# Operands of the seven products without the norm's root, two plain tiles, and two pairs of tiles in 256-column passes

## The chip, the cores and the metric

One NeuronCore of a Trainium2 chip runs the whole program. The metric is the device time of one execution in microseconds (us); lower is better. Engines are named as the profile names them: PE (TensorE, matmuls), PEld (its weight loads), DVE (VectorE), ACT (ScalarE), POOL (GpSimd) and SP (SyncE, which issues most transfers).

## What is computed

A block of two layers on 512 tokens of width 1024. Each layer has a feed-forward, a mixer (attention in the first, Mamba-2 in the second) and a second feed-forward, so that four feed-forwards run, numbered 0 to 3. The reference, cut:

```python
def rms_norm(x, g):
    y = x * lax.rsqrt(jnp.mean(x * x, axis=-1, keepdims=True) + EPS)
    return y * g

def swiglu(x, w_gate, w_up, w_down):
    return (jax.nn.silu(x @ w_gate) * (x @ w_up)) @ w_down

for i in range(2):
    x = x + 0.5 * swiglu(rms_norm(x, ffn1_norm[i]), ffn1_w_gate[i], ffn1_w_up[i], ffn1_w_down[i])
    h = rms_norm(x, mix_norm[i])
    x = x + (moba_mixer(h, ...) if i == 0 else mamba2_mixer(h, ...))
    x = x + 0.5 * swiglu(rms_norm(x, ffn2_norm[i]), ffn2_w_gate[i], ffn2_w_up[i], ffn2_w_down[i])
```

All is float32. The hidden width of a feed-forward is 2816 = 22 tiles of 128.

## The kernel before

**Layout.** x lies in SBUF as eight tiles x0 to x7 of 128 features by 512 tokens. A float32 product is made of three faster matmuls: each operand is split into a high part in the format fp32r and the rest (hi and lo), and hi x hi, hi x lo and lo x hi are added in PSUM. ACT makes hi (a copy, `high`), DVE makes lo (a subtraction, `low`). That holds for weights too: they come from DRAM into nine buffers of 128 x 1024 (`wraw`), and `halve_weights` splits each unit into `whi` and `wlo`, of which four of each exist.

**A plain tile** of a feed-forward (`plain`) makes gate and up of 128 hidden features: 8 tiles of K, times 2, times 3 matmuls of 512 columns. Its moving operands are `xhi` and `xlo`, which are x times the norm's gain; the norm's root r is put on the results, in `gated`.

**A pair** of tiles (`pair`) uses a scheme of Strassen's kind: the two tiles' gate and up weights, two halves of K, and two halves of the 512 tokens form 2 x 2 blocks, and seven products (A11, A12, A21-A22, -S2, A12-S2, A11-A21, A22) take the place of eight. Sums of weights are made by accumulating transfers that POOL issues (`add_term`, wraw<-wgu and wraw<-wraw). Sums of x are made on DVE by `Norm.spread` and `combined` (xa, xb, xd, xe) and split by `sided` into tiles `side`, which hold hi in 256 columns and lo in the next 256. A product runs in two passes: the weight's hi with all 512 columns of `side`, which leaves two parts in two PSUM banks that are added later, and the weight's lo with the first 256. The results are joined in tiles c1, c2, c4 and c5 (`read`, `joined`), and `gate` forms silu(gate) times up.

**Order.** Feed-forward i handles the first tiles as plain ones (six in feed-forward 0, four in the others, `GROUPS[i][0]`), then groups of two or three pairs. Between the products of a group's pairs stand the down-products (`down`) of the group before: eight, one for each x tile. The last group's down-products end the feed-forward; each adds to an x tile, after which `Norm.add` starts the next norm's work on that tile. `Norm.finish` sums the squares on PE, takes the power on POOL, and spreads r over the partitions as `rb` (PE, then ACT). In the kernel before, the operands of the pairs are scaled by r as well, so that `spread` begins with

```python
yield When(lambda: self.rb is not None)
```

**What sets the order of the instructions.** The program is put in order when it is built, by `Scheduler`: it keeps a clock for each engine and an estimated cost for each operation, and always places next the operation that could start first, ties going to the lower rank. The main line (tiles, pairs, mixers) is one task on PE, whose order is fixed. All engines run their lists in order. `Q.norm` is true from the seventh sum of squares until r is there, and a new accumulating transfer is not begun in that time; one that had passed this test earlier may still be placed in it. Weights are loaded in the order of the list `jobs`.

Of the kernel before, what the change touches and what calls it, by code (L numbers as in the profile page):

```python
# [25 lines left out]
KT = D // 128  # L26
# [17 lines left out]
ATTN = (("qk", 0), ("v", 0), ("qk", 1), ("qk", 2), ("qk", 3), ("v", 1), ("wo", 0), ("wo", 1))  # L44

SSM = (("x", 0), ("z", 0), ("x", 1), ("z", 1), ("x", 2), ("z", 2), ("x", 3), ("z", 3), ("out", 0), ("x", 4), ("z", 4), ("x", 5), ("z", 5),
       ("x", 6), ("x", 7), ("z", 6), ("z", 7), ("out", 1), ("out", 2), ("out", 3))
# [108 lines left out]
class Scheduler:  # L156
# [188 lines left out]
def trunk(ctx, tc, xT, pos, consts, cols, rows, wgu, wd, wqk, wv, wo, win, wz, wdt, wout, outT):  # L345
# [10 lines left out]
    sizes = {"slot": 53, "hs": 12, "sq": 6, "tiny": 40, "wraw": 9, "whi": 4, "wlo": 4}  # L356
# [67 lines left out]
    def ffn_order(i):  # L424

        order = list(range(*GROUPS[i][0]))
        for g in range(1, len(GROUPS[i])):
            a, b = GROUPS[i][g]
            pairs = [(j, j + 1) for j in range(a, b, 2)]
            n = 0  # L430
            for m, pair in enumerate(pairs):
                downs = []
                while n < KT * (m + 1) // len(pairs):
                    downs.append(("down", g - 1, n))
                    n += 1
                order.append((pair, downs))
        return order + [("down", len(GROUPS[i]) - 1, n) for n in range(KT)]
# [7 lines left out]

    def pair_jobs(i, pair, downs):

        (b11, b21), (b12, b22) = ((wgu[i, j, :, :1024], wgu[i, j, :, 1024:]) for j in pair)
        right = {"A11": (b11, None), "A12": (b21, None), "A21-A22": (b12, b11), "-S2": (b22, "A21-A22"),
                 "A12-S2": (b22, None), "A11-A21": (b12, b22), "A22": (b21, "-S2")}  # L450
        for nm in pair_order(downs):
            if isinstance(nm, tuple):
                down_job(i, nm)
            else:
                src, term = right[nm]
                job(src, step=2.78, total=2.78, whole=True, term=term, name=nm)

    def pair_order(downs):
        rest = iter(downs)
        order = [next(rest, None) if nm is None else nm for nm in PAIR]  # L460
        return [nm for nm in order if nm is not None] + list(rest)

    for l in range(2):
        for i in (2 * l, 2 * l + 1):
            if i == 1:
                for what, c in ATTN:
                    if what == "wo":
                        job(wo[c, 0])
                        job(wo[c, 1])
                    else:  # L470
                        wide_jobs(wqk[c] if what == "qk" else wv[c])
            if i == 3:
                for what, n in SSM:
                    if what == "x":
                        job(win[n, 0])
                        job(win[n, 1])
                    elif what == "z":
                        job(wz[n])
                    else:
                        job(wout[n, 0])  # L480
                        job(wout[n, 1])
# [134 lines left out]
    class Norm:  # L616


        def __init__(self, gain):
            self.gain = gain  # L620
# [4 lines left out]
            self.plain, self.spread_left = 0, 8  # L625
            self.left = {nm: [None] * 4 for nm in PAIR if nm}

        def add(self, k, first=False):
            self.there += 1
            spawn(self.operand(k), URGENT - 1 if first else 10 + k)  # L630
            spawn(self.square(k, first), 9 if k == KT - 1 and not first else 30 + k)
# [18 lines left out]
        def spread(self):  # L650


            yield When(lambda: self.rb is not None)
            for k in range(4):
                xa, xb = yield [slot("xa"), slot("xb")]
                Q.uses[xa.tensor.name] = Q.uses[xb.tensor.name] = 4
                for t, kk in ((xa, k), (xb, k + 4)):
                    op = V.scalar_tensor_tensor(t, x[kk], self.gain[:, kk:kk + 1], self.rb, op0=OP.mult, op1=OP.mult)
                    yield op.frees(*([self.rb] if kk == 7 and not self.plain else []))
                self.spread_left -= 2  # L660
                spawn(self.sided("A11", k, xa[:, :256], xa), 60)
                spawn(self.sided("A12", k, xb[:, :256], xb), 61)
                spawn(self.sided("A22", k, xb[:, 256:], xb), 66)
                spawn(self.combined(k, xa, xb), 62)

        def combined(self, k, xa, xb):
            d = yield slot("xd")
            Q.uses[d.tensor.name] = 4
            yield V.tensor_tensor(d[:, :256], xa[:, 256:], xb[:, 256:], op=OP.subtract).frees(xa, xb)
            spawn(self.sided("A21-A22", k, d[:, :256], d), 62)  # L670
            yield V.tensor_tensor(d[:, 256:], d[:, :256], xa[:, :256], op=OP.subtract).frees(xa, d)
            spawn(self.sided("-S2", k, d[:, 256:], d), 63)
            e = yield slot("xe")
            Q.uses[e.tensor.name] = 2
            yield V.tensor_tensor(e[:, :256], xb[:, :256], d[:, 256:], op=OP.add).frees(xb, d)
            spawn(self.sided("A12-S2", k, e[:, :256], e), 64)
            yield V.tensor_tensor(e[:, 256:], xa[:, :256], xa[:, 256:], op=OP.subtract).frees(xa)
            spawn(self.sided("A11-A21", k, e[:, 256:], e), 65)
# [63 lines left out]
    def ffn(i, nrm, done, midway=None):  # L742
        spawn(nrm.finish(), URGENT - 1)
        spawn(nrm.spread(), 60)
        h = {}

# [6 lines left out]
        def gated(pg, pu, j):  # L753
# [5 lines left out]
            nrm.plain -= 2  # L759
            yield op.frees(*([] if nrm.plain or nrm.spread_left else [nrm.rb]))  # L760
# [30 lines left out]
        def pair(j0, j1, downs, last):  # L791
# [12 lines left out]
            out = {}  # L804

            def product(nm, ps, first):
                p = place[nm]
# [17 lines left out]

            def parts(ps):
                v = ps.rearrange("p (o h c) -> p o h c", o=2, h=2)
# [5 lines left out]
            def gate(j, t, src):  # L833
                if j not in out:
# [3 lines left out]
                a = out[j][0][:, 256 * t:256 * t + 256]  # L838
                yield S.activation(a, src[:, :256], AF.Silu)
# [5 lines left out]
            def read(ps, nm, box):  # L845

                hh, hl = parts(ps)
                t = yield slot(nm)
                yield S.activation(both(t), hl, AF.Copy)
                yield V.tensor_tensor(both(t), hh, both(t), op=OP.add)  # L850
                box[nm] = t

            def joined(ps, nm, box, sign, done):
# [3 lines left out]
                for m, part in enumerate(parts(ps)):  # L857
# [4 lines left out]
                    yield op.frees(*([ps] if m and done else []))  # L862
# [16 lines left out]
            def c21(x):  # L879
                hh, hl = parts(x)  # L880
# [6 lines left out]
            for nm in order:  # L887
# [4 lines left out]
                elif nm == "A11":  # L892
                    x_ = yield bank("px", 2)
                    yield from product(nm, x_, True)
                    spawn(read(x_, "c1", box), 6)
                elif nm == "A12":
                    z_ = yield bank("pz", 2)
                    yield from product(nm, z_, True)
                    spawn(c11(z_), 6)
                elif nm == "A21-A22":  # L900
                    y_ = yield bank("py", 2)
# [36 lines left out]
        for what in ffn_order(i):  # L938
            if isinstance(what, int):
                yield from plain(what, what == GROUPS[i][0][1] - 1)  # L940
# [47 lines left out]
    def attention(nrm, done):  # L988
# [126 lines left out]
        def project(c, last):  # L1115

            for m in range(2):
                p = take(wo[c, m])
                for o in range(4):
# [4 lines left out]
                    for k in range(4):  # L1124
# [4 lines left out]
                        if n == KT - 1:  # L1129
# [11 lines left out]
        values_of = {0: {}, 1: {}}  # L1141
        for what, c in ATTN:
            if what == "wo":
                yield from project(c, c == 1)
# [9 lines left out]
    def mamba(nrm, done):  # L1154
# [79 lines left out]
        scaled_left = [6 * G]  # L1234

# [156 lines left out]
        def project(b, last):  # L1392

            for m in range(2):
                p = take(wout[b, m])
                for o in range(4):
# [4 lines left out]
                    for k in range(4):  # L1401
# [4 lines left out]
                        if n == KT - 1:  # L1406
# [20 lines left out]
        for i, (what, n) in enumerate(SSM):  # L1427
# [15 lines left out]
            else:  # L1443
                yield from project(n, n == 3)
# [23 lines left out]
    norms = [Norm(g) for g in gains]  # L1468
    for i, m in enumerate((0, 2, 3, 5)):
        norms[m].plain = 2 * GROUPS[i][0][1]  # L1470
# [105 lines left out]
```

## Time and profile before

| | |
|---|---|
| median of 3 runs | 2020.22 us (2019.89 to 2020.79) |
| the profiled execution | 2020.6 us, span on the core 2018.8 us, granted TensorE clock 1.00 |
| instructions | 28279 |
| matmuls | 10404 |
| DMA | 332.35 MB, mean 165 GB/s |

In the timeline by stages, feed-forward 0 runs to about 350 us, attention to 573, feed-forward 1 to 914, feed-forward 2 to 1257, Mamba to 1673, feed-forward 3 to the end. A row of groups gives the engine, the operation, the result and its sources by name, the shapes, the number of instructions, then the busy time, the mean duration of one in ns, and idle time of the engine ahead of them with what ended it. A row in order of time gives start, duration, instruction, and in brackets the idle time ahead of it. Rows of waits give total, count and longest.

### The profile page before, as it was taken

What the parts mean: (1) busy time and instruction counts of PE and PEld (TensorE: products, weight loads), DVE (VectorE), ACT (ScalarE), POOL (GpSimd) and SP (SyncE); (2) the same over time, 40 slices, a digit from 0 to 9 for tenths busy, and PEclk for the clock granted to TensorE, in tenths of its full rate; (3) what the DMA queues carried; (4) which work ended last, traced back from release to release, by engine and by line L of the source; (5) the groups of instructions that cost most, each with busy time, mean ns of one, the idle gap of its engine ahead of it and who ended that gap; (6) DMA issues with size and microseconds to landing.
All of it is one profiled execution on the core that took longest, in us unless ns stands there. A gap on an engine that the chain in (4) does not pass through costs nothing.

```text
span 2018.8 us, 28279 instructions
## 1 busy us (share of the span) xinstructions
PE 2012.8 (100%) x10404; PEld 1699.6 (84%) x10404; DVE 1501.5 (74%) x2251; ACT 1070.5 (53%) x1805; POOL 433.9 (21%) x402
## 2 busy tenths in 40 slices
PE   9999999999999999999999999999999999999999
PEld 7888888888888888888888888888888888888887
DVE  7977777668778777767877776676677777877774
ACT  6544445465654444544444454787477635444452
POOL 1203111334031111112111101254344422111110
PEclk9999999999999999999999999999999999999999
DMA  7678884221237888854888884143334334788881
GB/s 260 176 195 214 227 223 156 95 79 48 76 103 191 229 222 225 226 170 115 209 228 217 234 225 147 66 126 92 107 100 99 105 115 111 206 226 223 237 219 63
DMA packets 105979, 332.35 MB, mean 165 GB/s; under 512 B 11888, under 2 KB 13040, under 8 KB 105840
## 3 DMA queue, kind: packets, MB, share of 16 engines
q1 hardware_dynamic: 85392, 256.88, 39.5%
q0 software_dynamic: 20160, 73.41, 20.5%
q8 instruction: 82, 1.34, 0.3%
q14 instruction: 57, 0.47, 0.1%
q10 hardware_dynamic: 288, 0.25, 0.0%
HBM read 291.63 MB, written 2.16 MB: 146 GB/s over the span
## 4 chain that ended last, share of the span: by engine, by line
PE 98%; DVE 1%; DMA 1%; issue 0%; ACT 0%; POOL 0%; DVEq 0%; POOLq 0%
PE banks L230 98%; DMA wraw<-wgu 1%; DVE rstd L230 0%; DVE mx L230 0%; DVE ropea L230 0%; DVE qklo L230 0%; DVE wlo L230 0%; DVE ropeb L230 0%; POOL r L230 0%; ACT whi L230 0%; DVE banks L230 0%; POOL wraw L230 0%; DVE rs_a L230 0%; ACT qkhi L230 0%; ACT sq L230 0%
## 5 line engine op out<-in xcount | busy, mean ns | idle before, releaser
L230 ACT ACTIVATE whi<-wraw 128x1024 fp32r<-128x1024 f32 (+3 forms) x540 | 506.4, 939 | 518.7 <-PE banks L230 247.1
L230 DVE TENSOR_TENSOR wlo<-wraw,whi 128x1024 fp32r<-128x1024 f32 (+3 forms) x540 | 589.1, 1092 | 130.5 <-ACT whi L230 124.7
L230 PE MATMUL banks<-side,whi 128*128 128x512 f32 x1960 | 478.7, 392 | 0.0
L230 PEld LDWEIGHTS banks<-side,whi 128*128 128x128 f32 x1960 | 360.2, 188 | 79.3 <-DVE c L230 6.7
L230 PE MATMUL banks<-hhi,whi 128*128 128x512 f32 x704 | 275.2, 391 | 0.0
L230 PE MATMUL banks<-hlo,whi 128*128 128x512 f32 x704 | 275.1, 391 | 0.0
L230 PE MATMUL banks<-hhi,wlo 128*128 128x512 f32 x704 | 273.8, 389 | 0.0
L230 PEld LDWEIGHTS banks<-side,wlo 128*128 128x128 f32 x1960 | 258.0, 191 | 13.9
L230 PE MATMUL banks<-xhi,whi 128*128 128x512 f32 x672 | 268.1, 399 | 0.0
L230 PE MATMUL banks<-xhi,wlo 128*128 128x512 f32 x672 | 262.5, 391 | 0.0
L230 PE MATMUL banks<-side,wlo 128*128 128x256 f32 x1960 | 262.2, 282 | 0.0
L230 PE MATMUL banks<-xlo,whi 128*128 128x512 f32 x672 | 260.8, 390 | 0.0
L230 DVE TENSOR_TENSOR c<-banks,c 128x512 f32<-128x512 f32 x280 | 192.4, 687 | 83.0 <-PE banks L230 49.3
L230 DVE SCALAR_TENSOR_TENSOR x<-banks,x 128x512 f32<-128x512 f32 (+1 forms) x161 | 110.3, 686 | 69.5 <-PE banks L230 69.0
L230 POOL DMA_DIRECT2D wraw<-wraw x70 | 61.6, 880 | 449.7 <-DMA wraw<-wgu 199.4
L230 PEld LDWEIGHTS banks<-hhi,wlo 128*128 128x128 f32 x704 | 132.2, 188 | 28.3
L230 PEld LDWEIGHTS banks<-hhi,whi 128*128 128x128 f32 x704 | 132.5, 188 | 24.9
L230 POOL DMA_DIRECT2D wraw<-wgu x70 | 63.2, 902 | 415.3 <-DMA wraw<-wgu 171.8
L230 PEld LDWEIGHTS banks<-hlo,whi 128*128 128x128 f32 x704 | 132.6, 188 | 23.5
L230 PEld LDWEIGHTS banks<-xhi,whi 128*128 128x128 f32 x672 | 126.8, 189 | 26.9 <-ACT sq L230 0.8
L230 PEld LDWEIGHTS banks<-xhi,wlo 128*128 128x128 f32 x672 | 126.3, 188 | 26.7
L230 PEld LDWEIGHTS banks<-xlo,whi 128*128 128x128 f32 x672 | 126.3, 188 | 25.7
(212 smaller groups left out, 2660.1 us busy)
## 6 DMA issues: line engine op xcount, KB each, us to landing
wraw<-wgu SPq DMA_DIRECT2D x279, 512.0 KB, 4.8
wraw<-wgu POOLq DMA_DIRECT2D x70, 512.0 KB, 8.6
wraw<-wraw POOLq DMA_DIRECT2D x70, 512.0 KB, 6.1
wraw<-wd SPq DMA_DIRECT2D x128, 256.0 KB, 4.9
wraw<-win SPq DMA_DIRECT2D x32, 512.0 KB, 3.7
wraw<-wd SPq DMA_DIRECT2D x32, 384.0 KB, 3.8
wraw<-wqk SPq DMA_DIRECT2D x16, 512.0 KB, 4.2
wraw<-wz SPq DMA_DIRECT2D x16, 512.0 KB, 3.7
```

Of the source, the lines that this page charges most:

```text
L230: op.fn(*op.args, **op.kw)
```

## The change

- Feed-forwards 1, 2 and 3 have two plain tiles instead of four (`PLAIN`); tiles 2 and 3 become a pair without down-products, whose products stand in an order of their own (`QUAD`). Feed-forward 0 keeps six.
- The operands of the pairs are made of x times the gain, without r, by ACT. In feed-forwards 1 to 3 they begin as soon as two x tiles are there. r is put on gate and up in `gate`, by one more DVE operation for each half of a tile; `gate` becomes a task of its own with rank 30.
- The pairs that begin at tiles 2 and 4 in feed-forwards 1 to 3 (`SINGLE`) run in three passes of 256 columns into one PSUM bank (`product_single`), so that their parts needn't be added.
- The halves of K are the even and the odd tiles instead of the first and the last four.
- While `Q.norm` is true, the scheduler places no accumulating transfer at all.
- The projections of attention and Mamba are listed in halves. The numbers of buffers change.

```diff
+PLAIN = (6, 2, 2, 2)
+SINGLE = {(i, j) for i in (1, 2, 3) for j in (2,4)}
...
-                if isinstance(task.want, list) and isinstance(task.want[0], Op):
+                if isinstance(task.want, list) and isinstance(task.want[0], Op) and not (self.norm and task.gen.__name__ == "add_term"):
...
-    sizes = {"slot": 53, "hs": 12, "sq": 6, "tiny": 40, "wraw": 9, "whi": 4, "wlo": 4}
+    sizes = {"slot": 58, "hs": 9, "sq": 5, "tiny": 16, "wraw": 9, "whi": 4, "wlo": 4}
...
-        order = list(range(*GROUPS[i][0]))
+        order = list(range(PLAIN[i])) + [((j, j + 1), []) for j in range(PLAIN[i], GROUPS[i][0][1], 2)]
...
+    QUAD = ("A11", "A12", "-S2", "A21-A22", "A11-A21", "A12-S2", "A22")
...
+            if self.plain:
+                spawn(self.operand(k), URGENT - 1 if first else 10 + k)
+            spawn(self.square(k, first), 9 if k == KT - 1 and not first else (30 if self.plain else 10.5) + k / 10)
+            if self.paired and k % 2 == 0:
+                spawn(self.spread(k // 2), self.rank("A11", k // 2))
...
+        def rank(self, nm, k):
+            return (60 if self.first else 11) + 2 * SIDES.index(nm) + 0.1 * k
+        def spread(self, k):
+            if self.first:
+                yield When(lambda: self.rb is not None)
+            xa, xb = yield [slot("xa"), slot("xb")]
+            yield S.activation(xa, x[2 * k], AF.Copy, scale=self.gain[:, 2 * k:2 * k + 1])
+            self.side("A11", k, xa[:, :256], xa)
+            yield When(lambda: self.there > 2 * k + 1)
+            yield S.activation(xb, x[2 * k + 1], AF.Copy, scale=self.gain[:, 2 * k + 1:2 * k + 2])
...
-                steps = [[(4 * u + kk, o, 2 * u + o, 128 * kk, kk == 3, (0, 1, 2))] for u in range(2) for o in range(2) for kk in range(4)]
+                steps = [[(2 * kk + u, o, 2 * u + o, 128 * kk, kk == 3, (0, 1, 2))] for u in range(2) for o in range(2) for kk in range(4)]
...
+            def product_single(nm, ps, first):
...
+                        ops = [PE.matmul(ps[:, c:c + 256], st, mv, start=first and o == k == m == 0, stop=k == 3 and m == 2, skip_group_check=True)
+                               for m, (st, mv) in enumerate(((hi, a[:, :256]), (hi, a[:, 256:]), (lo, a[:, :256])))]
...
             def gate(j, t, src):
+                spawn(gate_(j, t, src), 30)
...
+                yield When(lambda: nrm.rb is not None)
+                r = nrm.rb[:, 256 * t:256 * t + 256]
+                op = V.tensor_tensor(both(src), both(t_), r[:, None, :].to_broadcast([128, 2, 256]), op=OP.mult)
                 yield S.activation(a, src[:, :256], AF.Silu)
...
-    lo4, hi4 = slice(0, 4), slice(4, 8)
+    lo4, hi4 = slice(0, 8, 2), slice(1, 8, 2)
```

More of the change, by code (lines that the diff above doesn't have):

```diff
@@ L455, in pair_jobs @@
                 src, term = right[nm]
-                job(src, step=2.78, total=2.78, whole=True, term=term, name=nm)
+                job(src, step=2.78, total=2.78, whole=True, term=term)
     def pair_order(downs):
+        if not downs:
+            return QUAD
         rest = iter(downs)
@@ L624, in __init__ @@
             self.added = 0
[L625 removed]
+            self.uses = 0
             self.left = {nm: [None] * 4 for nm in PAIR if nm}
@@ L629, in add @@
             self.there += 1
-            spawn(self.operand(k), URGENT - 1 if first else 10 + k)
-            spawn(self.square(k, first), 9 if k == KT - 1 and not first else 30 + k)
+            if self.plain:
+                spawn(self.operand(k), URGENT - 1 if first else 10 + k)
+            spawn(self.square(k, first), 9 if k == KT - 1 and not first else (30 if self.plain else 10.5) + k / 10)
+            self.first = first
+            if self.paired and k % 2 == 0:
+                spawn(self.spread(k // 2), self.rank("A11", k // 2))
         def operand(self, k):
@@ L648, in square @@
             Q.norm = not first and self.added >= KT - 1
[L650 to L664, printed above, removed]
@@ L667, in combined, with second @@
             d = yield slot("xd")
             Q.uses[d.tensor.name] = 4
+            spawn(self.combined(k, xa, xb, d), self.rank("A21-A22", k))
+        def combined(self, k, xa, xb, d):
             yield V.tensor_tensor(d[:, :256], xa[:, 256:], xb[:, 256:], op=OP.subtract).frees(xa, xb)
-            spawn(self.sided("A21-A22", k, d[:, :256], d), 62)
+            self.side("A21-A22", k, d[:, :256], d)
+            spawn(self.second(k, xa, xb, d), self.rank("-S2", k))
+        def second(self, k, xa, xb, d):
@@ L677, in combined, with fourth, side @@
+        def fourth(self, k, xa, e):
             yield V.tensor_tensor(e[:, 256:], xa[:, :256], xa[:, 256:], op=OP.subtract).frees(xa)
-            spawn(self.sided("A11-A21", k, e[:, 256:], e), 65)
+            self.side("A11-A21", k, e[:, 256:], e)
+        def side(self, nm, k, src, t):
+            spawn(self.sided(nm, k, src, t), self.rank(nm, k))
         def sided(self, nm, k, src, *done):
@@ L758, in gated @@
             op = GP.tensor_tensor(a, a, nrm.rb, op=OP.mult)
-            nrm.plain -= 2
-            yield op.frees(*([] if nrm.plain or nrm.spread_left else [nrm.rb]))
+            nrm.uses -= 1
+            yield op.frees(*scaled())
             yield V.tensor_tensor(a, pu, a, op=OP.mult).frees(pu)
@@ L804, in pair @@
             out = {}
+            single = (i, j0) in SINGLE
+            W = 1 if single else 2
             def product(nm, ps, first):
+                if single:
+                    yield from product_single(nm, ps, first)
+                    return
                 p = place[nm]
@@ L824, in product @@
                             yield op
+            def product_single(nm, ps, first):
+                p = place[nm]
+                Q.done_us = needed[p]
+                yield unit(p, 0)
+                un = units[p][0]
+                for o in range(2):
+                    for k in range(4):
+                        yield When(lambda: nrm.left[nm][k] is not None)
+                        a = nrm.left[nm][k]
+                        b, c = 512 * o + 128 * k, 256 * o
+                        hi, lo = cut(un, b, b + 128)
+                        ops = [PE.matmul(ps[:, c:c + 256], st, mv, start=first and o == k == m == 0, stop=k == 3 and m == 2, skip_group_check=True)
+                               for m, (st, mv) in enumerate(((hi, a[:, :256]), (hi, a[:, 256:]), (lo, a[:, :256])))]
+                        if o and k == 3:
+                            ops[-1].frees(*un)
+                        if last and o:
+                            ops[-1].frees(a)
+                        yield ops
             def parts(ps):
+                if single:
+                    return (both(ps),)
                 v = ps.rearrange("p (o h c) -> p o h c", o=2, h=2)
@@ L845, in read @@
             def read(ps, nm, box):
-                hh, hl = parts(ps)
                 t = yield slot(nm)
-                yield S.activation(both(t), hl, AF.Copy)
-                yield V.tensor_tensor(both(t), hh, both(t), op=OP.add)
+                if single:
+                    yield S.activation(t, ps, AF.Copy)
+                else:
+                    hh, hl = parts(ps)
+                    yield S.activation(both(t), hl, AF.Copy)
+                    yield V.tensor_tensor(both(t), hh, both(t), op=OP.add)
                 box[nm] = t
@@ L861, in joined @@
                         op = V.tensor_tensor(both(t), part, both(t), op=OP.add if sign == 1 or m else OP.subtract)
-                    yield op.frees(*([ps] if m and done else []))
+                    yield op.frees(*([ps] if m == W - 1 and done else []))
             box = {}
@@ L879, in c21 @@
             def c21(x):
+                if single:
+                    yield from gate(j0, 1, x)
+                    return
                 hh, hl = parts(x)
@@ L939, in ffn @@
             if isinstance(what, int):
-                yield from plain(what, what == GROUPS[i][0][1] - 1)
+                yield from plain(what, what == PLAIN[i] - 1)
             elif what[0] == "down":
@@ L1113, in head, with project @@
             oT[n] = (hi, lo)
-        def project(c, last):
-            for m in range(2):
+        def project(cm, c, last, seen):
+            for m in (cm % 2,):
                 p = take(wo[c, m])
+                seen.add(cm)
                 for o in range(4):
@@ L1390, in joined, with project @@
                 ys[t] = pair
-        def project(b, last):
-            for m in range(2):
+        def project(bm, b, last, seen):
+            for m in (bm % 2,):
                 p = take(wout[b, m])
+                seen.add(bm)
                 for o in range(4):
```

66 lines of the change are left out of this document (40 added, 26 removed).

## The prediction

> **What bounds the kernel now.** I read the page's busy line first, then its chain, then the waits of PE.
>
> ```profile
> PE 2012.8 (100%) x10404; PEld 1699.6 (84%) x10404; DVE 1501.5 (74%) x2251; ACT 1070.5 (53%) x1805; POOL 433.9 (21%) x402
> ...
> PE 98%; DVE 1%; DMA 1%; issue 0%; ACT 0%; POOL 0%; DVEq 0%; POOLq 0%
> ```
> ```profile
> PE banks L230 <- DVE warm L1448: 1.2, 1, 1.2
> PE banks L230 <- DVE r L230: 0.9, 1, 0.9
> ```
>
> PE fills the span, and after the start it waits once, 0.9 us, for the norm's root r. But ends of matmuls are modelled, so "busy" alone doesn't say that PE can't go faster. The pace shows in start times. I therefore looked at stretches of one kind: plain tiles alone, two whole groups of pair plus four down-products, and, in order of time, the matmuls of one pair.
>
> ```profile
> 584.00:616.00 32.00, 32.00 (x143) 26.50 (x142) 29.08 (x54) 19.98 (x40) 5.99 (x5) 1.00 0.37 90
> 679.00:740.00 61.00, 61.00 (x322) 52.35 (x321) 45.69 (x63) 28.83 (x43) 6.96 (x8) 1.00 0.88 226
> ```
> ```profile
> 650.30 2.08 PE L230 MATMUL banks<-side,wlo 128*128 128x256 f32 x16
> 652.21 3.82 PE L230 MATMUL banks<-side,whi 128*128 128x512 f32 x16
> 655.87 1.35 PE L230 MATMUL banks<-side,wlo 128*128 128x256 f32 x10
> ```
>
> (Columns of the first fence: stretch and length, then PE, PEld, DVE, ACT and POOL busy, granted clock, DMA share, GB/s.) Some 141 matmuls of 512 columns start in 32.00 us (143 are listed, two of them across the edges): 0.227 us each. Sixteen of 256 columns take 652.21 - 650.30 = 1.91 us: 0.119 to 0.120 each. The next sixteen of 512 take 3.66 us instead of 16 x 0.227 = 3.63, so a switch of width costs about 0.03. At these paces nothing is lost between matmuls. The time is PE's count of columns, plus what PE is made to wait. Both must be summed.
>
> **Part 1: columns.** A plain tile is 48 matmuls of 512: 48 x 0.227 = 10.9 us. A pair in two passes: (61.00 - 96 x 0.227) / 2 = 19.6 us (the 96 are the eight down-products of 12). A pair in 256-column passes is 7 products x 24 matmuls = 168 x 0.120 = 20.2, with switches 20.25. In each of feed-forwards 1 to 3, two plain tiles go (2 x 10.9), one new 256-column pair comes (tiles 2, 3), and one pair (4, 5) goes from 19.6 to 20.25. Sum: 6 x 20.25 - 6 x 10.9 - 3 x 19.6 = 121.5 - 65.4 - 58.8 = -2.7 us. Bounds: a pace of 0.119 or 0.121 moves it by 1.0 either way, so -3.7 to -1.7. The projections of attention and Mamba are listed in halves, but in the old order: 0. In feed-forward 0 the six plain tiles stay.
>
> What a 256-column pass rests on is the weight load in front of each matmul, now 24 a product instead of 16:
>
> ```profile
> L230 PEld LDWEIGHTS banks<-side,wlo 128*128 128x128 f32 x1960 | 258.0, 191 | 13.9
> ```
>
> A load lasts 0.191 us, yet matmuls follow every 0.120, so loads overlap running matmuls and each other over runs of 16. I take it that 168 in a row go as 16 do. [...]
>
> **Part 2: the one wait.**
>
> ```profile
> 913.06 0.90 POOL L230 DMA_DIRECT2D wraw<-wgu  x1 [2.83 <-DVE wlo L230]
> 913.67 1.62 POOL L230 TENSOR_TENSOR acc<-acc,sq 128x512 f32<-128x512 f32 x1
> 921.78 0.88 POOL L230 DMA_DIRECT2D wraw<-wraw  x1 [6.49 <-DMA wraw<-wgu]
> 922.39 1.33 POOL L230 TENSOR_TENSOR r<-ms,mhalf 128x4 f32<-128x4 f32 x1
> ```
> ```profile
> 923.12 0.39 PE L230 MATMUL banks<-xhi,wlo 128*128 128x512 f32 x1
> 924.37 0.65 PE L230 MATMUL banks<-cc,r 128*128 128x128 f32 x4 [0.86 <-DVE r L230]
> ```
>
> At the start of feed-forward 2, POOL holds an accumulating weight transfer that waits 6.49 us for another's landing, and the root's power stands behind it on POOL. PE then starts 924.37 - 923.12 - 0.227 = 1.0 us late. The scheduler's new condition never places such a transfer while a norm is being closed, so this goes: -1.0. The transfer comes after the power instead. Bounds: -1.0, and +1.0 if a transfer placed just before the norm closes holds POOL in another feed-forward. I take -1.0. The same condition delays the 12 added transfers by the norm's length, which the nine raw units cover (rival C).
>
> **Part 3: work on DVE and ACT, hidden behind PE while they keep up.** Durations:
>
> ```profile
> L230 DVE TENSOR_TENSOR wlo<-wraw,whi 128x1024 fp32r<-128x1024 f32 x375 | 467.3, 1247 | 95.3 <-ACT whi L230 90.4 <-DMA wraw<-wgu 0.2
> L230 DVE TENSOR_TENSOR c<-banks,c 128x512 f32<-128x512 f32 x280 | 192.4, 687 | 83.0 <-PE banks L230 49.3 <-ACT c L230 33.2
> L230 DVE TENSOR_TENSOR hlo<-ga,hhi 128x512 fp32r<-128x512 f32 x88 | 62.3, 709 | 13.7 <-ACT hhi L230 13.6 <-PE banks L230 0.2
> L230 DVE TENSOR_TENSOR ga<-c,ga 128x256 f32<-128x256 f32 x140 | 59.6, 426 | 34.0 <-ACT ga L230 34.0
> L230 DVE SCALAR_TENSOR_TENSOR xa<-x,colp,rb 128x512 f32<-128x512 f32 x16 | 15.1, 941 | 3.6 <-ACT rb L230 3.6
> L230 DVE SCALAR_TENSOR_TENSOR xb<-x,colp,rb 128x512 f32<-128x512 f32 x16 | 11.9, 745 | 0.0
> ```
>
> Added: the root on gate and up, four 512-column DVE operations a pair, 38 x 4 x 0.687 = 104 us. Taken off: the scaling of x, 27.0 us (to ACT as 32 copies); in each 256-column pair that was a two-pass pair, seven sums or joins of 0.687, 14.4 us in all. The three exchanged pairs add 21 - 12 = 9 weight units x 1.25 and less gating, some 11 to 15. DVE goes from 1501 to about 1575 us, 78%. In the steady groups it goes from 45.69 / 61.00 = 75% to (45.69 + 8 x 0.687) / 61.00 = 84%. Cost on the path: 0, because PE covers it; the cover ends near full occupancy.
>
> The place where little cover is left is the first pair. Before, 45 us of plain tiles lie between the last x and it; after, some 23. Against that, operands no longer wait for r: they start with x0 and x1, in the stretch where x comes out. DVE and ACT there, then during the first plain tiles, then the operand halves alone (DVE, during the first pair):
>
> ```profile
> 546.00:573.00 27.00, 27.00 (x121) 22.36 (x120) 16.72 (x22) 13.18 (x20) 9.44 (x7) 1.00 0.34 92
> 573.00:618.00 45.00, 45.00 (x206) 37.37 (x205) 36.82 (x67) 23.89 (x46) 8.76 (x8) 1.00 0.44 113
> ```
> ```profile
> 618.00:680.00 62.00, 3.15 (x9) 1.00 0.82 214
> ```
>
> The 36.82 of DVE shrink by two tiles (4 x 1.25 + 6 x 0.69 = 9.1) and by the scaling (6): 21.7 for 23 us, and 10.3 us are idle in the 27 before. So the operands for the first products are ready. During the 20.2 us of the first pair DVE has 7 x 1.25 + 7 x 0.687 + 4 x 0.426 + 2 x 0.709 = 16.7 us, and 19.9 if the same nine halves come late. That fits, with a share up to 98%. ACT, at 50 to 55%, takes the 32 copies. I put small waits here and along the fuller DVE at +0.4 (0 to +7, rival B).
>
> At the end of a feed-forward the root lengthens the chain behind the last product:
>
> ```profile
> 879.05 0.60 ACT L230 ACTIVATE c<-banks 128x512 f32<-128x512 f32 x1
> ...
> 883.37 0.69 DVE L230 TENSOR_TENSOR hlo<-ga,hhi 128x512 fp32r<-128x512 f32 x1
> ...
> 884.54 0.39 PE L230 MATMUL banks<-hlo,whi 128*128 128x512 f32 x1
> ```
>
> hlo is finished at 884.06 and used at 884.54: 0.48 us spare. The new operation takes 0.69, so up to 0.2 is waited for, more if another DVE operation slips in front, in three feed-forwards. I take +0.4 (0 to +2).
>
> The new halves of K (even and odd tiles) make plain tiles want x6 at the fourth step, 9 x 0.227 = 2.0 us in, instead of the second half of the weights. Its last operand:
>
> ```profile
> 571.90 0.75 DVE L230 SCALAR_TENSOR_TENSOR xlo<-x,colp,xhi 128x512 fp32r<-128x512 f32 x1 [0.80 <-ACT xhi L230]
> ...
> 572.93 0.39 PE L230 MATMUL banks<-xhi,whi 128*128 128x512 f32 x1
> ```
>
> It is there at 572.65 and wanted at 572.93 + 2.0 = 574.97: 2.3 us spare, and the pair's earlier operands now rank ahead of it on ACT and DVE. I take 0; bound +1 for each of three.
>
> **Sum:** -2.7 - 1.0 + 0.4 + 0.4 = -2.9. The profiled execution took 2020.6 us (span 2018.8) and becomes 2017.7; it stands 0.4 above the median of 2020.22, so the median becomes 2017.3, -0.14%. A measurement of this kernel can tell about 0.2%, 4.0 us: 2016.2 is the edge of faster, 2024.3 that of slower.
>
> **Rivals.** *A, clearly faster:* no new waits, and 256-column matmuls at 0.119: -3.7 - 1.0 = -4.7, so 2015.5. For it: PE waits nowhere else now, and steady groups have had idle DVE. Against: every chain gets longer.
>
> *B, slower: DVE becomes the bound in the first pair.* The fullest stretch without a PE wait now is 36.82 / 45 = 82%; if DVE can't get past 87% there, 19.9 us of work take 22.9 instead of 20.2: 2.7 each, 8 for three feed-forwards: 2020.22 - 2.9 + 8 = 2025.3. It decides once more than about 1 us of operand work is left over at the pair's start at that share. Against: 10.3 us idle ahead of it.
>
> *C, slower: weights arrive late for the first pair.* It asks for seven loads and four accumulating transfers:
>
> ```profile
> wraw<-wgu SPq DMA_DIRECT2D x279, 512.0 KB, 4.8
> wraw<-wgu POOLq DMA_DIRECT2D x70, 512.0 KB, 8.6
> wraw<-wraw POOLq DMA_DIRECT2D x70, 512.0 KB, 6.1
> ```
>
> That is 11 x 0.524 = 5.77 MB in 20.2 us, 286 GB/s; the groups reach 226 at a share of 0.88, at most 257. Without a reserve: 22.5 us, +2.3 each, 7 in all, 2024.2 or a little over. Against: nine raw units are filled during plain tiles at a share of 0.37 to 0.44.
>
> *D, the change doesn't bring its columns:* x6 or the operands are late by what the tiles saved, 0.9 us each: about 2020.
>
> *E, loads that don't overlap:* 384 x 0.191 = 73 us, 2090. Every row above speaks against it. [...]
>
> **How the numbers follow.** Forecast 0.45 (2017.3; its own range 2016.2 to 2019), A 0.30, D 0.08, B 0.12, C 0.04, E 0.01. Faster is A; same is the forecast and D; slower is B, C, E: 0.30, 0.53, 0.17. The range goes from 2014.8 (A with both ends of the columns) to 2023.5 (into B): some 0.15 is left out, most of it above.
>
> **What would show it.** In the new profile: PE's waits without r; 256-column matmuls 0.120 apart through 168 of them; plain stretches of about 22 us; a first pair of 20.2 us; DVE near 1575 us and about 84% in groups. Wrong if PE's starts show gaps in the first pair (B: behind DVE side; C: behind whi or wlo), at the fourth step of a plain tile (D), or at the last down-products' hlo.

## The result, and the profile after

The changed kernel is slower. Of its first five executions one was disturbed and took 5172 us, and the profile had fallen on it; the other four have a median of 2031.47 us (2029.06 to 2034.97) against 2020.69, a ratio of 1.0054 [1.0042, 1.0066]. The same kernel was therefore run again. The repeat gave 2027.17 us (2026.38 to 2032.35) against 2021.22, ratio 1.0034 [1.0021, 1.0047], with a profiled execution of 2032.35 us (span 2030.6). That profile is the "after" of this document, and it is the slowest of its five executions; why it is 5 us above the median is part of the answer. Forecast were 2017.3 and a range up to 2023.5.

The busy line and PE's waits after (waited in all, how often, the longest):

```profile
PE 2013.1 (99%) x10788; PEld 1721.1 (85%) x10788; DVE 1576.1 (78%) x2368; ACT 1099.7 (54%) x1858; POOL 434.6 (21%) x408
```
```profile
PE banks L232 <- DVE acc L232: 4.7, 2, 2.4
PE banks L232 <- DVE xlo L232: 3.9, 3, 1.5
PE banks L232 <- DVE wlo L232: 3.7, 1, 3.7
```

DVE's 1576 us is what was forecast. The wait for r is gone, and three others stand in its place: for the norm's sum (acc), for the low half of an x tile (xlo), for the low half of a weight (wlo). Now stretches of time: 256-column matmuls in ffn 2, from behind the root's matmuls in the first pair on into the second; the first 20.2 us of that, as long as one pair; the steady groups; and in the last fence three short stretches at or behind waits of PE.

```profile
949.54:982.37 32.83, 32.83 (x276) 32.83 (x274) 24.93 (x34) 19.28 (x29) 6.04 (x6) 1.00 0.79 202
949.54:969.76 20.22, 20.22 (x171) 20.22 (x169) 16.79 (x24) 13.04 (x19) 5.18 (x5) 1.00 0.80 191
```
```profile
679.00:740.00 61.00, 61.00 (x323) 52.63 (x322) 50.71 (x71) 28.50 (x42) 6.97 (x8) 1.00 0.91 226
```
```profile
173.39:176.80 3.41, 3.41 (x13) 2.93 (x12) 2.97 (x4) 1.23 (x2) 0.00 (x0) 0.50 0.70 206
613.71:617.12 3.41, 3.41 (x19) 3.41 (x18) 1.66 (x4) 1.54 (x2) 1.77 (x2) 0.50 0.55 99
580.00:583.40 3.40, 1.86 (x9) 1.22 (x8) 3.40 (x8) 3.40 (x7) 0.71 (x2) 1.00 0.36 135
```

The 256-column matmuls keep 0.120 us through a whole pair and beyond (276 are listed, some three of them across the edges: 32.83 / 273), DVE has 16.79 us of work in that stretch of 20.2 us (16.7 was forecast for a pair) and is at 50.71 / 61 = 83% in the groups. The column term came out as worked out. The last fence has what was not: behind the waits for wlo and acc PE runs 3.41 us at a granted clock of 0.50. In the first of these stretches down-products start 0.43 us apart (174.46 to 176.60 us, five steps) instead of 0.227. I estimate that each wait costs 1.7 us more than its length, half of 3.41. Behind the wait of 1.54 us for xlo, in the third row, the clock was 1.00.

**The wait for xlo** is x6 at the fourth step of the first plain tile. DVE and PE, in order of time, in ffn 1:

```profile
575.55 0.69 DVE L232 TENSOR_TENSOR x<-banks,x 128x512 f32<-128x512 f32 x1 [0.41 <-PE banks L232]
...
577.16 1.22 DVE L232 TENSOR_TENSOR wlo<-wraw,whi 128x1024 fp32r<-128x1024 f32 x1
...
580.57 0.76 DVE L232 TENSOR_TENSOR side<-xd,side 128x256 fp32r<-128x256 f32 x2
581.24 0.75 DVE L232 SCALAR_TENSOR_TENSOR xlo<-x,colp,xhi 128x512 fp32r<-128x512 f32 x1
```
```profile
580.11 0.39 PE L232 MATMUL banks<-xhi,whi 128*128 128x512 f32 x1
582.04 0.50 PE L232 MATMUL banks<-xlo,whi 128*128 128x512 f32 x1 [1.54 <-DVE xlo L232]
```

x6 is written from 575.55 on, but its xlo only runs at 581.24. Between them DVE does x5's low half, a weight half, x7, and eight operand pieces of the pairs (side, xd) that rank from 11 where x6's operand has rank 16. PE starts 582.04 - 580.11 - 0.227 = 1.70 us late; in ffn 2 it is 0.97, in ffn 3 1.70, in sum 4.4.

**The wait for acc** lies inside the first pair: the four column sums of the squares, which give the root.

```profile
601.65 1.06 ACT L232 ACTIVATE whi<-wraw 128x1024 fp32r<-128x1024 f32 x1 [3.86 <-PE banks L232]
...
606.07 0.62 ACT L232 ACTIVATE sq<-x 128x512 f32<-128x512 f32 x1
...
608.43 0.90 POOL L232 DMA_DIRECT2D wraw<-wraw  x1 [5.88 <-issue]
...
609.03 1.58 POOL L232 TENSOR_TENSOR acc<-acc,sq 128x512 f32<-128x512 f32 x1
610.65 0.69 DVE L232 TENSOR_TENSOR acc<-acc,sq 128x512 f32<-128x512 f32 x1 [3.71 <-POOL acc L232]
...
611.40 1.05 PE L232 MATMUL banks<-ones,acc 128*128 128x1 f32 x8 [2.38 <-DVE acc L232]
```

The last square comes out of ACT at 606.69, 28 us after x7 (578.97). A square has rank 30, and every operand piece of the pairs ranks ahead of it. ACT wasn't full for all that: it runs its list in order, and in the first of these rows it idles 3.86 us in front of a weight half that has to wait for PE, with two squares behind it.

But the last square is not what the sum waits for. The seventh is out at 603.23, and POOL has been free since 602.55. In POOL's list an accumulating transfer stands ahead of the seventh addition; it issues at 608.43, after 5.88 us of idle time, and only then come POOL's addition and DVE's eighth, which has idled 3.71 us for it. Behind the last square alone the eighth addition would have been done at about 607.4 (606.69 and 0.69), and PE wanted it at 608.9. Feed-forward 3 repeats this: the last square is out at 1709.89, the transfer issues at 1711.57 behind 5.96 us of idle time, and PE is free at 1712.1. So late squares leave little to spare, and the transfer makes the wait. No run takes that transfer away alone. By its starts PE is 2.5 us late in ffn 1 and again in ffn 3, and each time 3.41 us at half clock follow.

**The wait for wlo** is in feed-forward 0, which the change leaves alone in its products. POOL and DVE:

```profile
168.04 4.84 DVE L232 TENSOR_TENSOR wlo<-wraw,whi 128x1024 fp32r<-128x1024 f32 x1
...
170.76 0.68 POOL L232 TENSOR_TENSOR ropesin<-sin,rowp 128x128 f32<-128x128 f32 x1
```

Here POOL makes the rotary tables, 18 operations in a row from 163.64 to 172.25, and beside them a subtraction on DVE takes 4.84 us that takes 1.23 elsewhere. PE starts 3.9 us late.

**One gain had not been foreseen.** Before, PE's weight loads waited for c 29 times; PE's own row of waits doesn't list these. Before, then after:

```profile
PEld banks L230 <- DVE c L230: 6.7, 29, 0.3
```
```profile
PEld banks L232 <- DVE c L232: 0.4, 1, 0.4
```

What moved is the order on ACT. Before the change, and behind it the same place after:

```profile
686.77 0.42 ACT L230 ACTIVATE ga<-c 128x256 f32<-128x256 f32 x1 [1.36 <-DVE c L230]
687.09 1.04 ACT L230 ACTIVATE whi<-wraw 128x1024 fp32r<-128x1024 f32 x1
...
688.17 1.23 DVE L230 TENSOR_TENSOR wlo<-wraw,whi 128x1024 fp32r<-128x1024 f32 x1 [0.52 <-ACT whi L230]
...
689.31 0.68 DVE L230 TENSOR_TENSOR c<-banks,c 128x512 f32<-128x512 f32 x1
```
```profile
696.39 1.06 ACT L232 ACTIVATE whi<-wraw 128x1024 fp32r<-128x1024 f32 x1 [1.18 <-PE banks L232]
696.57 0.69 DVE L232 TENSOR_TENSOR c<-c,rb 128x512 f32<-128x512 f32 x1
...
697.48 1.23 DVE L232 TENSOR_TENSOR wlo<-wraw,whi 128x1024 fp32r<-128x1024 f32 x1 [0.22 <-ACT whi L232]
697.83 0.41 ACT L232 ACTIVATE ga<-c 128x256 f32<-128x256 f32 x1
698.62 0.68 DVE L232 TENSOR_TENSOR c<-banks,c 128x512 f32<-128x512 f32 x1
```

Before, the Silu (ga) goes ahead of the weight's high half, so wlo and then c come later, and the next product's load waits 0.2 us. After, the product by the root stands in front of the Silu, and whi passes it. Two-pass pairs start their down-products 14.00 us after the pair's first load (718.93 to 732.93 in the trace after) instead of 14.08 (709.20 to 723.28 before); over 29 such pairs that is 2.3 us.

So the span's 2030.6 - 2018.8 = +11.8 is: columns -2.7, r -1.0, loads -2.3, xlo +4.4, acc +5.0, wlo +3.9, half clock 3 x 1.7 = +5.1; together +12.4, 0.6 too much. Without the clash in feed-forward 0 and its half clock (3.9 + 1.7) this span would be 6.2 longer than before, and the median is 6.0 longer: the profiled execution seems to have met the clash where the median one did not.

### The profile page after: what moved, and what is told of

Read it like the earlier page. It is cut to its first block, busy times and chain, and to the rows that moved or that the text cites. A ratio compares the mean times of both kernels' runs of the same rounds, so it can differ in the third digit from the quotient of the medians.

```text
span 5170.3 us, 29269 instructions
## 1 busy us (share of the span) xinstructions
PE 5165.3 (100%) x10788; PEld 3452.2 (67%) x10788; DVE 1558.2 (30%) x2368; ACT 1115.7 (22%) x1858; POOL 415.3 (8%) x408
## 4 chain that ended last, share of the span: by engine, by line
PE 100%; DVE 0%; DVEq 0%; issue 0%
PE banks L232 100%; DVE x L232 0%; DVEq L1647 0%; DVE warm L1525 0%
## 5 line engine op out<-in xcount | busy, mean ns | idle before, releaser
L232 PE MATMUL banks<-side,whi 128*128 128x512 f32 (+1 forms) x2464 | 1381.5, 747 | 0.0
L232 PEld LDWEIGHTS banks<-side,whi 128*128 128x128 f32 x2464 | 880.7, 380 | 402.5 <-issue 400.9
L232 PEld LDWEIGHTS banks<-side,wlo 128*128 128x128 f32 x2128 | 710.9, 413 | 77.0 <-issue 76.8
L232 PE MATMUL banks<-side,wlo 128*128 128x256 f32 x2128 | 748.0, 529 | 0.0
L232 PE MATMUL banks<-hhi,whi 128*128 128x512 f32 x704 | 575.7, 818 | 0.0
L232 PE MATMUL banks<-hlo,whi 128*128 128x512 f32 x704 | 575.2, 817 | 0.0
L232 PE MATMUL banks<-hhi,wlo 128*128 128x512 f32 x704 | 574.0, 815 | 0.0
L232 PE MATMUL banks<-xhi,whi 128*128 128x512 f32 x576 | 489.9, 851 | 0.0
L232 PE MATMUL banks<-xhi,wlo 128*128 128x512 f32 x576 | 476.6, 827 | 0.0
L232 PE MATMUL banks<-xlo,whi 128*128 128x512 f32 x576 | 474.4, 827 | 0.0
```

Source lines behind the costliest of these rows:

```text
L232: op.fn(*op.args, **op.kw)
```

## The experiments

Each edit is to the changed kernel unless said otherwise. The lines shown are PE's waits of that kernel.

**Plain tiles back, no 256-column passes (plain4).**

```
-PLAIN = (6, 2, 2, 2)
-SINGLE = {(i, j) for i in (1, 2, 3) for j in (2,4)}
+PLAIN = (6, 4, 4, 4)
+SINGLE = set()
```

> The change with four plain tiles in feed-forwards 1 to 3 and no 256-column pairs: operands without the root, the root on gate and up, the new halves of K, the scheduler's condition and the new buffer counts stay. The columns on PE are those of the kernel before. Theories B and C: the cover is back, so the loss goes, 2019 to 2021 us. Theory F: the loss stays, 2030 us or more.

Measured 2022.99 us (2021.79 to 2026.18), ratio 1.001 [1.0, 1.0019]: 1.8 above the kernel before, just outside what was expected. With four plain tiles the wait for acc is gone, and two waits for x6 stay:

```profile
PE banks L232 <- DVE xlo L232: 3.1, 2, 1.5
```

So the late norm belongs to the fewer tiles, and the late x6 comes whatever the tiles. That the ranks make it late is shown by x_first below. That the new halves of K have a part in it, by asking for x6 earlier, is argued; no run changes them alone.

**The tiles taken away, the new pair in two passes (twopass).** SINGLE = set(), PLAIN as changed.

> The change with two plain tiles, but with all pairs in two passes. PE has 6 x 0.65 = 4 us less to do than in the changed kernel, DVE has 6 x 7 x 0.687 = 29 us more, close around the first pairs. Theory B: slower than the changed kernel by 5 us or more. Theory C: about the same gaps, so about 4 us faster or the same. Theory F: about 4 us faster.

Measured 2063.18 us (2059.97 to 2063.83), ratio 1.0204 [1.0187, 1.0221].

```profile
PE banks L232 <- DVE c L232: 11.2, 7, 2.6
PE banks L232 <- DVE hlo L232: 9.2, 3, 5.9
PE banks L232 <- ACT hhi L232: 7.4, 3, 4.0
```

These three rows alone are 27.8 us, all of work behind products. The expected cost is there; that DVE's full load makes it is true only in part. Around the longest wait DVE itself stands still:

```profile
643.18 0.88 POOL L232 DMA_DIRECT2D wraw<-wraw  x1 [7.14 <-DMA wraw<-wgu]
...
645.39 0.69 DVE L232 TENSOR_TENSOR ga<-banks,ga 128x512 f32<-128x512 f32 x1 [3.72 <-POOL ga L232]
```

POOL's product for a plain tile's gate (643.75 to 645.36) stands behind the transfer, as the sum of squares did in the changed kernel, and DVE is busy for 10.26 of the 20 us from 640. Six stretches at half clock, 34 us in all, cost some 17 us besides (the mean clock of that execution is 0.992). Two-pass pairs this early are costly; how much of that is DVE's load (rival B), this run doesn't tell.

**The x operands ranked ahead (x_first).**

```
-                spawn(self.operand(k), URGENT - 1 if first else 10 + k)
+                spawn(self.operand(k), URGENT - 1 if first else 10 + k / 10)
```

> The changed kernel with the operands of plain tiles ranked ahead of the operands of pairs (10 + k / 10 in place of 10 + k). Theory R (order: x6's operand comes late only because pair operands rank ahead of it): PE's three waits for xlo (1.5, 1.5 and 0.9 us in the trace of the changed kernel) go, -4 us, the waits for acc stay; about 2023 us. Theory S (DVE is simply too full around the first pair): the waits turn up behind side or c in the first pair, time unchanged within 1 us.

Measured 2035.46 us (2028.94 to 2038.55), ratio 1.0064 [1.0043, 1.0086]. Expected was a gain; the kernel is 8 us slower than the changed one. The waits for xlo are gone, and others have come, with the clash of feed-forward 0 (wlo 3.1) beside them:

```profile
PE banks L232 <- DVE hlo L232: 5.2, 3, 2.7
PE banks L232 <- DVE acc L232: 3.6, 2, 2.1
```

No pair piece is late at the wait for hlo: DVE works on none between 616 and 641 us. The root is late. Its first product on DVE runs at 619.64, and the hlo that PE waits for at 640.99. In both_first, which differs only in the squares' rank, the same two run at 610.72 and 634.62.

**The squares ranked ahead (squares_first).** For the norms of feed-forwards 1 to 3:

```
-            spawn(self.square(k, first), 9 if k == KT - 1 and not first else (30 if self.plain else 10.5) + k / 10)
+            spawn(self.square(k, first), 9 if k == KT - 1 and not first else (30 if self.plain and (first or not self.paired) else 10.8) + k / 100)
```

> The changed kernel with the squares of the norm ranked ahead of the operands of pairs (10.8 in place of 30) in feed-forwards 1 to 3. Theory R: the sums of squares are there before the first pair, PE's two waits for acc (2.4 us each) and the 3.4 us at half clock behind each go: 2 x (2.4 + 1.7) = -8 us; about 2019 us. Theory S: the 8 squares and 8 sums only push other operands back, time unchanged within 2 us.

Measured 2036.33 us (2031.12 to 2038.04), ratio 1.0072 [1.0057, 1.0087]. It was expected to gain and is 9 us slower than the changed kernel, with 17 us at half clock (mean clock 0.996) and the clash (3.7) in its trace. Now the x operands stand behind the squares as well:

```profile
PE banks L232 <- DVE xlo L232: 7.4, 3, 2.9
...
PE banks L232 <- DVE acc L232: 2.3, 2, 1.3
```

**Both orders (both_first).** The two edits together.

> Both edits of ranks. Theory R: -12 us, 2015 us, faster than both kernels; it stays above 2014.8, which is the columns' gain and POOL's wait with nothing lost. Theory S: 2022 us or more, with waits behind side in the first pairs.

Measured 2017.93 us (2015.51 to 2021.73), ratio 0.9987 [0.9978, 0.9997]. After the start one wait of PE is left, the clash of feed-forward 0:

```profile
PE banks L232 <- DVE wlo L232: 3.7, 1, 3.7
```

Either edit alone moved the waits; both put the work in the order in which PE asks for it: x, then the norm, then the pair's pieces. DVE's total work lies between 1574.8 and 1579.4 us in all three and in the changed kernel, so what was short was not DVE's time but its order. In this kernel the last sum of squares in ffn 1 is done at 580.42 and PE takes it at 582.15; the next accumulating transfer, at 584.64, comes behind it.

**The kernel before, gate as a task of its own and the new condition (before_gate).** To the kernel before:

```
+                spawn(gate_(j, t, src), 30)
+                yield When(lambda: True)
...
-                if isinstance(task.want, list) and isinstance(task.want[0], Op):
+                if isinstance(task.want, list) and isinstance(task.want[0], Op) and not (self.norm and task.gen.__name__ == "add_term"):
```

> The kernel before, with two small parts of the change alone: the gate as a task of its own with rank 30 (without the root's multiplication), and the scheduler's condition on accumulating transfers. By the traces of weight loads, 35 pairs lose 0.07 us each to a wait for c before and none after: -2.5 us. The wait for r at 924 us goes: -1.0 us. Together 2017.5 us, all of it without touching a column. If the two are not the cause of what was gained, the time stays within 0.5 us of the kernel before.

Measured 2020.41 us (2020.11 to 2021.70), ratio 0.9997 [0.9988, 1.0007]. Expected was 2017.5; it is 0.5 below the kernel before, within the noise. The wait for r is gone, but new waits for xhi of 1.0 us take its place, and the loads still wait for c:

```profile
PEld banks L230 <- DVE c L230: 7.3, 32, 0.3
```

So the condition does what it says, and the separate task is not what took the loads' waits away.

**The same with a product by ones ahead of each Silu (before_ones).**

```
+                quarters = src.rearrange("p (q c) -> p q c", q=4)
+                yield V.tensor_tensor(quarters, quarters, ones[:, None, :].to_broadcast([128, 4, 128]), op=OP.mult)
                 yield S.activation(a, src[:, :256], AF.Silu)
```

> The kernel before with the gate as a task of its own and the scheduler's condition (that took 2020.41), plus one DVE product of 128x512 by ones ahead of each Silu, some 140 x 0.69 = 96 us of DVE work that changes no value. Theory O (in the kernel before, Silu is put ahead of the next whi on ACT, so wlo and then c come 0.2 to 0.3 us late and the weight load in front of a product waits 29 times; the added operation in front of Silu turns that order round): PE's weight loads no longer wait for c (6.7 to 7.3 us in total before), 2.5 us faster, 2018, unless the last down-products' hlo takes back up to 0.6. Rival (other parts of the change took these waits away, such as the buffer counts): the waits for c stay, and it takes 2020.4 to 2022.

Measured 2033.18 us (2030.56 to 2038.43), ratio 1.0064 [1.0052, 1.0077].

```profile
PE banks L230 <- DVE side L230: 7.9, 7, 1.5
PE banks L230 <- DVE wlo L230: 3.3, 1, 3.3
```
```profile
PEld banks L230 <- DVE c L230: 0.4, 1, 0.4
```

The loads' 7.3 us fall to 0.4: the order on ACT is the cause, as read from the rows. The time was a miss: 2018 was expected. The expectation looked for trouble at the last hlo, and it came at the pairs' operands (side), which in this kernel are still made after the root, at the clash (wlo), and in four stretches of 3.41 us at half clock, 6.8 us lost (mean clock 0.996). With the loads' -2.3 that makes 15.7 us of the 16.3 that the span grew. That more work behind the products leaves DVE no room for operands made late, so that the root on gate and up needs operands made early, fits these rows but was not tried by itself.

**The rotary tables on DVE (ropes_dve).** both_first, and

```
-                    yield GP.tensor_tensor(ta[:, :, w, 64 * o:64 * o + 64], cs_, same, op=OP.mult)
-                    yield GP.tensor_tensor(tb[:, :, w, 64 * o:64 * o + 64], sn, other, op=OP.mult)
-            op = GP.tensor_scalar(tb[:, :, :, 0:64], tb[:, :, :, 0:64], -1.0, None, op0=OP.mult)
+                    yield V.tensor_tensor(ta[:, :, w, 64 * o:64 * o + 64], cs_, same, op=OP.mult)
+                    yield V.tensor_tensor(tb[:, :, w, 64 * o:64 * o + 64], sn, other, op=OP.mult)
+            op = V.tensor_scalar(tb[:, :, :, 0:64], tb[:, :, :, 0:64], -1.0, None, op0=OP.mult)
```

> The kernel with both orders changed, and beside it the 18 products for the rotary tables (16 of 128x128, two sign changes of 128x256) made on DVE instead of POOL. Theory P (the burst of those products on POOL holds DVE's subtraction: wlo took 4.84 us there instead of 1.23): the one wait of PE left, wlo 3.7 us near 168.8, and the half clock behind it, 1.7 us lost, go; the products cost DVE 18 x some 0.2 us at the lowest rank, hidden. Span 2019.9 - 1.8 - 3.7 - 1.7 is about 2012.5, time about 2014.3 (ratio 0.997), and the repeats within 1 us of each other. Rival (that clash is not POOL's doing, the order of DVE alone makes wlo late there): the wait stays, 2016 to 2022 as before.

Measured 2015.49 us (2014.88 to 2016.43) against 2021.07, ratio 0.997 [0.9959, 0.9982]: faster than both kernels. The longest wait after the start is now 0.6 us, and the repeats lie within 1.6 us, where both_first spread over 6.2.

```profile
PE banks L232 <- DVE x L232: 0.6, 1, 0.6
```

**Only the first of the two pairs in 256-column passes (one_pass).** ropes_dve with SINGLE = {(i, 2) for i in (1, 2, 3)}.

> As the kernel with both orders changed and the tables on DVE, but only the pair of tiles 2 and 3 goes in 256-column passes; tiles 4 and 5 go in two passes as in the kernel before. By columns alone: 3 x 0.65 = 2.0 us less, so some 2012.3. Theory D (DVE's work around the first pairs decides; with two-pass pairs in both places the kernel took 43 us more than before): seven DVE operations of 0.687 more in each second pair make DVE late there, PE waits for c and hlo, 3 to 15 us slower than with both pairs, 2017 to 2030.

Measured 2027.52 us (2026.67 to 2028.58), ratio 1.0032 [1.002, 1.0043]: 2.0 us fewer columns, 12 us slower.

```profile
PE banks L232 <- ACT hhi L232: 5.6, 2, 3.6
```

Both pairs in 256-column passes are needed. Here DVE's load is plain: from 622 to 637 us, around the longest waits, it is busy for 13.49 of 15 us. Two stretches at half clock cost 3.4 us of the 12 (mean clock 0.998).

**A run of products on POOL elsewhere (pool_burst).** ropes_dve, with 18 products of 128x128 added on POOL in the middle of feed-forward 1:

```
+            op = GP.tensor_tensor(t[:, :128], q_gain, k_gain, op=OP.mult)
```

> The fastest kernel so far (both orders changed, rotary tables on DVE) with 18 products of 128x128 on POOL added in the middle of feed-forward 1, into a scratch tile; no value of the result changes. Theory P (a run of products on POOL holds a DVE operation with two operands in SBUF until the run is over): one DVE operation there (wlo or the product by the root) takes 2 to 8 us instead of 0.7 to 1.25, the next product waits for its operand, PE 1 to 6 us late, some 2017 to 2023 against 2015.5. Rival (POOL does not touch DVE; in the earlier place the order of DVE alone was at fault): every DVE operation keeps its 0.69 to 1.25 us beside the run, 2015.5.

Measured 2015.40 us (2014.72 to 2016.41), ratio 0.9972 [0.9962, 0.9982]. The theory that a run on POOL always holds DVE to its end fell: none of the eight executions is long. POOL, and DVE beside it:

```profile
674.46 7.78 POOL L232 TENSOR_TENSOR burst<-rowp 128x128 f32<-128x128 f32 x10
```
```profile
676.04 1.37 DVE L232 TENSOR_TENSOR wlo<-wraw,whi 128x1024 fp32r<-128x1024 f32 x1
677.33 0.94 DVE L232 TENSOR_TENSOR c<-c,rb 128x512 f32<-128x512 f32 x1
678.20 0.68 DVE L232 SCALAR_TENSOR_TENSOR x<-banks,x 128x512 f32<-128x512 f32 x1
```

The products came in runs of ten, one and seven. Beside the run of ten, DVE's operations that read no bank take 0.14 to 0.26 us longer (the subtraction 1.37 to 1.46 instead of 1.23, the product by the root 0.94 instead of 0.68) and those that read one keep their 0.68; beside the run of seven one subtraction kept 1.23 as well. PE waits nowhere for it. What makes a subtraction stand still for 4.84 us in feed-forward 0 is left open; that moving the tables off POOL ends it is shown (1.22 at 168.77 us in ropes_dve).

**The changed kernel with the tables on DVE alone (after_ropes).**

> The changed kernel as it is, with the rotary tables' 18 products on DVE and nothing else. Theory (three separate losses): the wait of 3.9 us near 168 and its 1.7 us at half clock go, the waits for x6 and for the norm's sum stay: 2026.4 in every repeat, spread under 2 us, ratio 1.003. Rival (the clash in feed-forward 0 is the greater part of the loss): 2021 or less.

Measured 2025.77 us (2024.68 to 2028.22), ratio 1.0023 [1.0014, 1.0033]. The spread of 3.5 us is more than the 2 that were expected. The wait for wlo is gone, the others stay:

```profile
PE banks L232 <- DVE acc L232: 3.5, 2, 1.8
PE banks L232 <- DVE xlo L232: 3.1, 2, 1.5
```

So the order of x, squares and pair pieces costs 2025.77 - 2015.49 = 10.3 us, more than the change's whole gain; the clash costs 2027.17 - 2025.77 = 1.4 us of the median, and some 5.6 in an execution in which it comes.

## Why the prediction was wrong

*The range.* Its lower end, 2014.8, doesn't follow from its terms: columns of -3.7 and -1.0 for r give 2015.5. Nothing hangs on it.

*Columns, -2.7: right.* The pace of 0.120 held through 168 and more, with loads of 0.190 to 0.192 us in the trace after; so rival E, in which each of the 384 added loads (10788 - 10404) costs its full length, is out. *The r wait, -1.0: right* (after, and before_gate). *DVE's share, 1575 us and 84% in groups: right* at 1576 and 83%. *Rival C: no wait for whi or wlo in the first pair.*

*"x6 at the fourth step ... I take 0; bound +1 for each of three": failed.* The step took the spare time of a trace in which x6 had no competitors, named the competitors, and priced them at nothing. Eight pieces of 0.4 us and a weight half lay in front: 1.70, 0.97 and 1.70 us. With the operands ranked ahead (x_first) the wait is gone. Rival D had the place and a smaller price.

*"Bounds: -1.0, and +1.0 if a transfer placed just before the norm closes holds POOL in another feed-forward. I take -1.0": failed.* What the bound describes came, in feed-forwards 1 and 3. The scheduler's new condition holds from the seventh sum of squares on, and the transfer stood just in front of that sum, in a list made from estimated costs. It cost 2.5 us twice. The prediction did not ask when squares of rank 30 would run once the pairs' pieces rank from 11: early sums would have left room for such a transfer, as in both_first. And behind each of these waits came 3.41 us at a clock of 0.50, 1.7 us lost by the estimate above. That a wait also costs clock was in no term; with the clash it is 5.1 us of this profile.

*The first pair, +0.4 (rival B as its price): the cause was another.* In ffn 1 and 3 DVE is busy for 13.6 and 13.3 of the 24 us of the first pair, in ffn 2 for 16.0 of 20.5: it did not bound them. The pair waited for the norm. Occupancy was summed where order had to be followed.

*The end of a feed-forward, +0.4: 0.* No wait for hlo or hhi there.

*Not in the sum:* the loads' waits for c (-2.3), visible in the rows of the weight loads and not read; and the clash in feed-forward 0 (+3.9, and 1.7 of half clock), which the prediction passed over because "in feed-forward 0 the six plain tiles stay": the order of the lists around them changed there too. Before, POOL made the tables in two runs (155 to 158 and 164 to 174 us), after, in one. One run is not enough for the clash, though: plain4 and twopass have one run too, and there PE's waits for wlo are 0.2 us and none. DVE's subtractions in plain4, and one of POOL's products beside them:

```profile
168.85 4.46 DVE L232 TENSOR_TENSOR wlo<-wraw,whi 128x1024 fp32r<-128x1024 f32 x4
...
172.19 1.44 POOL L232 TENSOR_TENSOR ropesin<-sin,rowp 128x128 f32<-128x128 f32 x1
```

Four subtractions take 4.46 us, hardly less than one in the trace after, and POOL's products take up to 1.44 us instead of 0.7. Five of the seven traces with one run have the clash. In the trace after and in both_first DVE's subtraction starts just after POOL's tenth operation (168.04 behind 167.85, 168.00 behind 167.79), in plain4 just before it (168.85 and 169.09). That is a pattern, not a cause shown: in pool_burst DVE began in the midst of a run and wasn't held.

With order and clash mended (ropes_dve) the gain was larger than forecast, -5.6 us against -2.9; columns, r and loads add up to -6.0.

## What to carry to other kernels

When work is moved to an earlier, fuller stretch, follow its order, not its sum: list what each engine will do between the last input and the first use, by rank, and see what falls behind. Two chains that compete must be mended together; mending one can only move the wait, and the single experiments then look as if the idea were wrong. Read the waits of the weight loads beside those of the matmuls, and price a wait of PE with what its clock does afterwards: in the trace after, 3.41 us at 0.50 behind three of its six waits after the start.

## What the runs showed of the hardware

A short wait of PE can be followed by a lower clock. In the trace after, PE ran 3.41 us at a granted clock of 0.50 from 173.39 us, behind the wait of 3.9 us for wlo, and again from 613.71 and 1716.21 us, behind the two waits for acc, where PE was 2.5 us late. The loss of 1.7 us each is an estimate, half of 3.41. Behind the wait of 1.54 us for xlo the clock was 1.00 (580.00 to 583.40). Length alone doesn't decide: of the two waits of 1.8 us for acc in after_ropes, one was followed by some 6.8 us at half clock (mean clock 0.52 from 606 to 613 us, 1.00 from 613 to 617), and around the other the mean clock was 1.00 (1700 to 1725). What decides is not shown.

Beside runs of products on POOL, DVE's operations took longer in some of these traces. In pool_burst the subtraction took 1.37 to 1.46 us instead of 1.23 and the product by the root 0.94 instead of 0.68, while the operation that reads a bank kept its 0.68. Which of the two engines takes longer, and by how much, was not steady: beside the tables one subtraction took 4.84 us and POOL's products kept 0.68 to 0.79 (after), or four subtractions took 4.46 us together and POOL's products up to 1.44 (plain4). Why is not shown. With the tables on DVE the repeats of both_first draw together from 6.2 to 1.6 us, so the clash is the likely source of that spread.
